# Half of the RWKV weight pieces split at use, low-rank outputs in two parts, other product rates

## Chip, cores and metric

The kernel runs on one core of a Trainium2 chip. The metric is device time in microseconds (us) of one execution. The profile shows one execution of the program: PE is the matmul engine (PEld its weight loads), DVE the vector engine, ACT the scalar engine, POOL GpSimd, and SP the engine whose queue issues most DMAs.

## What is computed

A two-layer trunk over 1024 tokens of width 1024, in float32. Layer 0 mixes tokens by a gated MLP (SGU), layer 1 by RWKV-7 time mixing; each is followed by a squared-ReLU MLP. Only the RWKV mixer and its products matter for the change:

```
xx = token_shift(h) - h
xr, xw, xk, xv, xa, xg = [h + xx * mu[i] for i in range(6)]
r, k, v = xr @ W_r, xk @ W_k, xv @ W_v             # "big": 1024 x 1024 each
w_log = -softplus(-(w0 + tanh(xw @ w1) @ w2)) - 0.5    # low rank: "hidden", then "outs"
a = sigmoid(a0 + (xa @ a1) @ a2)
g = sigmoid(xg @ g1) @ g2
y = wkv7_scan(r, exp(-exp(w_log)), k, v, -kk, kk * a)  # recurrence over tokens, 16 heads of 64
out = ((groupnorm(y) + bonus) * g) @ w_out          # "outp"
```

## The kernel before

**Three products for one.** Each float32 operand is split into a high part, rounded to the type fp32r, and a low part, the rest (`wh`, `wl` for weights). A product is high x high, high x low and low x high: three matmuls accumulate into one PSUM tile `acc`. A weight piece is one 128 x 512 tile (256 KB); twelve matmuls use it, two pieces make a block of eight row chunks.

**Where weight pieces come from.** `stream` lists the pieces in the order of use; `load_piece` loads up to three ahead; `split_piece` makes a piece ready, two pieces ahead of its use. There are two kinds. A raw piece is loaded as one tile `raw`, cast to `wh` (L401: two on ACT, the third on DVE) and subtracted to `wl` (L407: DVE and POOL in turn). A kept piece needs none of this: its two parts lie in DRAM (`split`), and `load_split` loads both (L326). The kept parts are made by `presplit` (L305 load, L355 cast on ACT, L358 subtraction on POOL, L336 two stores), step by step beside the layer-0 MLP. All 80 RWKV pieces are kept: 48 of r, k, v, 8 hidden, 8 outs, 16 of the output product.

**Stages of the RWKV mixer.** Tokens are worked in four quarters q of 256. `jobs` lists the products of a quarter: "big" products v, r, k, each in four parts m, with a hidden product behind m = 1 and all outs behind m = 2 (w beside v, a beside r, g beside k); after the four quarters come the output products "outp" of q = 0 and 1. The jobs of q = 0 run with raw pieces beside the end of the layer-0 MLP (about 1060 to 1220 us). All later ones run beside the recurrence (`wkv`), with kept pieces (1220 to 1810 us), followed by the first half of the layer-1 MLP with raw pieces, still beside the recurrence (to 2340 us).

**Results on their way.** Each job part m copies its PSUM tile into one of three `ev` buffers on ACT (L931 for big, L985 and L989 for outs) and ACT's queue stores it to DRAM (`sdr`, `sda`, ...). The recurrence loads these later. Only two PSUM tiles `acc` are open to products in this stage. When the output product of a quarter begins, `gated` loads its finished recurrence outputs (`ev<-yd`, L995) and splits them into `s`.

**The recurrence.** It has 16 units (4 quarters x 4 parts m). A unit moves its triangular matrix through DRAM: `ltd<-la`, `lb<-ltd` (L1412), a solve in many small DVE steps `pr`, `tb` (L1418 to L1424), `tpd<-tb` (L1428), `t<-tpd` and `pf<-tpd` (L1433). Then come twelve steps that depend on each other, of small PE matmuls `c`, DVE and ACT copies (`S` L1551, `uv` L1540, `xs` L1526).

**Order of the work.** `interleave` sets PE's order: each unit step has a due time in units; each piece of product work advances the clock by its cost over `RATES`, so 28.0 cost units of products lie in each of the first 10 units and 41.5 in each later one. PE keeps this order as written (`Pinned`); a scheduler sets the order on ACT, DVE, POOL and SP, and each of these works through its queue in order.

Of the kernel before, what the change touches and what calls it, by code (L numbers as in the profile page):

```python
# [16 lines left out]
P = 128  # L17
# [91 lines left out]
class Trunk:  # L109
# [148 lines left out]
    def std(self, src):  # L258

        return [(src[:, h * 4:h * 4 + 4], 1, None) for h in range(2)]  # L260
# [68 lines left out]
    def presplit(self, todo, pool):  # L329

        nc = self.nc
        got, out = [], iter(())

        def store(parts, ts, rows):
            for p, t in zip(parts, ts):
                nc.sync.dma_start(p[:rows], t[:rows])  # L336
                yield

        todo = list(zip(todo, self.split_ahead))
        for n in range(len(todo)):  # L340
            while len(got) < min(3, len(todo) - n):
                src, rep, _ = todo[n + len(got)][0]
                raw = pool.tile([P, 512], F32, name="araw", bufs=4)
                if rep:
                    k, m = src.shape[1:]
                    view = raw[:, :k * rep * m].rearrange("p (k r n) -> p k r n", k=k, r=rep)
                    self.fetch(view, src, rep)
                    rows = P
                else:
                    rows = self.fetch(raw, src, rep)[1]  # L350
                got.append((raw, rows))
            (raw, rows), ((_, _, low), (parts, _)) = got.pop(0), todo[n]
            m = parts[0].shape[-1]
            hi = pool.tile([P, 512], F32, name="ada_acc", bufs=2)
            nc.scalar.copy(hi[:rows, :m].bitcast(F32R), raw[:rows, :m])  # L355
            lo = slice(0, rows) if low is None else low
            to = raw if low is None else hi
            nc.gpsimd.tensor_tensor(to[lo, :m].bitcast(F32R), raw[lo, :m], hi[lo, :m], ALU.subtract)  # L358
            yield
            for _ in out:  # L360
                pass
            yield
            out = store(parts, (hi[:, :m], raw[:, :m]), rows)
            yield
        for _ in out:
            pass

    def make_split(self, dp):

        self.whole = [p for kind in ("big", "hidden", "outs", "outp")  # L370
                      for p in self.pieces(j for j in self.jobs() if j[1] == 0 and j[0] == kind)]
        kept = []
        for n, (src, rep, low) in enumerate(self.whole):
            m = src.shape[1] * rep * src.shape[2] if rep else 512
            rows = P if rep else sum(s.shape[0] for s in src)
            parts = [dp.tile([P, m], F32, name=f"split{n}_{i}") for i in range(1 if low else 2)]
            kept.append((parts, rows))
        self.split_ahead = kept
        at = lambda kind, q: [j for j in self.jobs() if j[:2] == (kind, q)]
        place, n = {}, 0  # L380
        for kind in ("big", "hidden", "outs", "outp"):
            for _, _, name, m in at(kind, 0):
                k = len(list(self.pieces([(kind, 0, name, m)])))
                place[kind, name, m] = slice(n, n + k)
                n += k
        self.order_split = [p for kind, _, name, m in self.parts()[1] for p in kept[place[kind, name, m]]]

    def split_piece(self):

# [420 lines left out]
    def jobs(self):  # L810


        for q in range(self.NQ):
            for name, low in ("vw", "ra", "kg"):
                for m in range(4):
                    yield "big", q, name, m
                    if m in (1, 2):
                        yield ("hidden", "outs")[m - 1], q, low, 0
        for q in range(2):
            for m in range(4):  # L820
                yield "outp", q, "", m
# [7 lines left out]
    def pieces(self, jobs):  # L829

        a = self.a
        std = self.std
        for kind, q, name, m in jobs:
            if kind == "big":
                for e in range(2 * m, 2 * m + 2):
                    yield from std(a["w_in"]["rkv".index(name) * 8 + e])
            elif kind == "outp":
                for e in range(2 * m, 2 * m + 2):
                    yield from std(a["b_w_out"][e])
            elif kind == "hidden":  # L840
                if name == "g":
                    yield from std(a["b_g1"][:, :, :P])
                    yield from [(a["b_g1"][:, h * 4:h * 4 + 4, P:], 3, None) for h in range(2)]
                else:
                    yield from [(a[f"b_{name}1"][:, h * 4:h * 4 + 4], 2, None) for h in range(2)]
            else:
                for h in range(2):
                    cs = slice(h * 512, h * 512 + 512)
                    if name == "g":
                        yield [a["b_g2"][:P, cs]], 0, None  # L850
                        yield [a["b_g2"][P:, cs]] * 3, 0, slice(64, 96)
                    else:
                        yield [a[f"b_{name}2"][:, cs]] * 2, 0, None

    def load_h(self, q):
        nc, N = self.nc, self.N
# [102 lines left out]
                nc.scalar.copy(gh[:96, 2], s[:96])  # L959
                nc.vector.tensor_tensor(gh[32:64, 2], s[32:64], rd(gh[32:64, 2]), ALU.subtract)  # L960

    def outs(self, q, name, _):
        nc = self.nc
        bias = {"w": self.w0h, "a": self.a0h, "g": None}[name]
        for m in range(4):
            if m % 2 == 0:
                wh, wl = self.piece()
                if name == "g":
                    gst, _ = self.piece()
            ps, half = self.acc2()  # L970
            for z in range(2):
                e = m % 2 * 2 + z
                es = slice(e * P, e * P + P)
                if name == "g":
                    gh = self.hid[:, 1:]
                    ops = (wh[:, es], gh[:, 0]), (wh[:, es], gh[:, 1]), (wl[:, es], gh[:, 0]), (gst[:96, es], gh[:96, 2])
                else:
                    ops = (wh[:, es], self.hid[:, 0]), (wl[:, es], self.hid[:, 0])
                for n, (w, x) in enumerate(ops):
                    self.pe.matmul(half[z], w, x, start=n == 0, stop=n == len(ops) - 1)  # L980
            yield 0.4 * len(ops)

            def emit(ev):
                if bias is None:
                    nc.scalar.copy(ev, ps)  # L985
                    return
                for z in range(2):
                    e = m * 2 + z
                    nc.scalar.activation(ev[:, z * self.N:(z + 1) * self.N], half[z], AF.Tanh, bias=bias[:, e:e + 1], scale=0.5)  # L989
            self.out2(q, name, m, emit)  # L990
# [191 lines left out]


    SLOT = 1 / 13
    RATES = [28.0] * 10 + [41.5]

    def wkv(self, bg):

# [605 lines left out]
```

## Time and profile before

| what | value |
|---|---|
| median of 3 runs | 2800.86 us (2793.97 to 2807.12) |
| profiled execution, its own time | 2805.26 us |
| its span, first to last instruction | 2803.5 us |
| busy in the span: PE | 2613.3 us, 93% |
| DVE, ACT, POOL | 1638.3, 1146.9, 544.7 us (58, 41, 19%) |
| DMA moved | 483.67 MB, mean 173 GB/s |
| mean granted clock of PE | 0.969 of full speed |

PE is busy for 93% of the span, so what counts is the other 7%, the time at a lower clock, and what ends PE's waits. The views used below are the table of busy time by stretch, the table of who waited for whom, the groups of instructions by line, the DMA issues with their median time from issue to landing, and single instructions in order of time.

### The profile page before, as it was taken

What the parts mean: (1) busy time and instruction counts of PE and PEld (TensorE: products, weight loads), DVE (VectorE), ACT (ScalarE), POOL (GpSimd) and SP (SyncE); (2) the same over time, 40 slices, a digit from 0 to 9 for tenths busy, and PEclk for the clock granted to TensorE, in tenths of its full rate; (3) what the DMA queues carried; (4) which work ended last, traced back from release to release, by engine and by line L of the source; (5) the groups of instructions that cost most, each with busy time, mean ns of one, the idle gap of its engine ahead of it and who ended that gap; (6) DMA issues with size and microseconds to landing.
All of it is one profiled execution on the core that took longest, in us unless ns stands there. A gap on an engine that the chain in (4) does not pass through costs nothing.

```text
span 2803.5 us, 49454 instructions
## 1 busy us (share of the span) xinstructions
PE 2613.3 (93%) x19020; PEld 2152.6 (77%) x19020; DVE 1638.3 (58%) x3066; ACT 1146.9 (41%) x2074; POOL 544.7 (19%) x574
## 2 busy tenths in 40 slices
PE   6999999999999999787898997879999999999998
PEld 4788888877888788787787886777777778788887
DVE  7856775444333458866666663566667545744445
ACT  4523442333311344553454543464444334533333
POOL 1000000433300013431322231123334220100001
PEclk9999999999999999998999999899999999999999
DMA  7644545888711354788888889753333324333332
GB/s 279 211 142 128 167 155 163 274 278 255 237 49 49 91 165 138 241 291 261 260 284 265 270 289 274 211 149 110 104 104 100 91 86 151 103 109 94 95 94 83
DMA packets 369708, 483.67 MB, mean 173 GB/s; under 512 B 144320, under 2 KB 153536, under 8 KB 368704
## 3 DMA queue, kind: packets, MB, share of 16 engines
q1 hardware_dynamic: 354496, 454.18, 52.3%
q10 hardware_dynamic: 14976, 26.34, 2.5%
q8 instruction: 149, 2.44, 0.4%
q14 instruction: 87, 0.71, 0.1%
HBM read 390.07 MB, written 90.32 MB: 171 GB/s over the span
## 4 chain that ended last, share of the span: by engine, by line
PE 67%; DVE 12%; DMA 11%; ACT 4%; issue 4%; SPq 1%; POOL 1%; ACTq 0%; DVEq 0%; POOLq 0%
PE acc L448 24%; PE acc L646 15%; PE acc L103 15%; PE c L103 2%; PE acc L503 2%; DMA split<-ada_acc 2%; PE t L103 2%; DMA split<-araw 2%; DVE pr L1420 2%; DVE hm L874 2%; PE acc L894 1%; DVE wl L407 1%; DMA araw<-in_ada_w 1%; DVE xi L440 1%; DMA lb<-ltd 1%
## 5 line engine op out<-in xcount | busy, mean ns | idle before, releaser
L448 PE MATMUL acc<-h,wh 128*128 128x512 f32 x2112 | 667.4, 397 | 0.0
L401 ACT CAST wh<-raw 128x512 fp32r<-128x512 f32 x517 | 318.6, 619 | 732.6 <-PE acc L448 299.0
L646 PE MATMUL acc<-s,wh 128*128 128x512 f32 (+1 forms) x1664 | 510.4, 389 | 12.1 <-DVE s L439 9.1
L407 DVE TENSOR_TENSOR wl<-raw,wh 128x512 fp32r<-128x512 f32 x475 | 363.1, 767 | 264.4 <-ACT wh L401 259.3
L448 PEld LDWEIGHTS acc<-h,wh 128*128 128x128 f32 x2112 | 394.9, 188 | 94.5 <-issue 1.2
L448 PE MATMUL acc<-h,wl 128*128 128x512 f32 x1056 | 418.0, 396 | 0.0
L646 PEld LDWEIGHTS acc<-s,wh 128*128 128x128 f32 x1664 | 308.9, 189 | 86.5 <-DVE s L439 14.8
L646 PE MATMUL acc<-s,wl 128*128 128x512 f32 (+1 forms) x832 | 323.1, 389 | 0.5 <-DVE wl L407 0.5
L452 DVE SCALAR_TENSOR_TENSOR x<-acc,mod,x 128x512 f32<-128x512 f32 (+1 forms) x224 | 163.1, 730 | 231.0 <-PE acc L646 206.4
L448 PEld LDWEIGHTS acc<-h,wl 128*128 128x128 f32 x1056 | 198.4, 188 | 48.0 <-issue 0.5
L103 PE MATMUL acc<-s,wh 128*128 128x512 f32 (+1 forms) x616 | 188.0, 390 | 35.0 <-ACT s L437 18.3
L407 POOL TENSOR_TENSOR wl<-raw,wh 128x512 fp32r<-128x512 f32 (+1 forms) x107 | 145.6, 1363 | 318.2 <-ACT wh L401 156.2
L103 PE MATMUL acc<-xi,wh 128*128 128x256 f32 (+1 forms) x896 | 179.5, 300 | 10.0 <-ACT hm L954 5.2
L646 PEld LDWEIGHTS acc<-s,wl 128*128 128x128 f32 x832 | 157.5, 189 | 35.3 <-DVE wl L407 1.2
L358 POOL TENSOR_TENSOR araw<-araw,ada_acc 128x512 fp32r<-128x512 f32 (+1 forms) x78 | 101.2, 1300 | 389.4 <-ACT ada_acc L355 354.1
L103 PEld LDWEIGHTS acc<-s,wh 128*128 128x128 f32 x616 | 111.0, 196 | 62.8 <-ACT s L437 18.8
L103 PEld LDWEIGHTS acc<-xi,wh 128*128 128x128 f32 (+1 forms) x896 | 144.3, 198 | 17.7 <-ACT hm L954 5.4
L103 PE MATMUL acc<-h,wh 128*128 128x512 f32 (+1 forms) x512 | 150.7, 381 | 3.2 <-ACT ev L1057 3.2
L103 PE MATMUL acc<-xi,wl 128*128 128x256 f32 (+1 forms) x448 | 129.8, 290 | 1.6 <-issue 0.8
L355 ACT CAST ada_acc<-araw 128x512 fp32r<-128x512 f32 (+1 forms) x80 | 49.4, 618 | 168.4 <-DMA split<-ada_acc 124.3
L103 PE MATMUL acc<-s,wl 128*128 128x512 f32 (+1 forms) x308 | 114.9, 373 | 0.0
L157 DVE SCALAR_TENSOR_TENSOR ada_acc<-araw,cond,ada_acc 128x512 f32<-128x512 f32 x140 | 104.4, 746 | 13.0 <-DMA araw<-in_ada_w 11.1
(269 smaller groups left out, 4415.8 us busy)
## 6 DMA issues: line engine op xcount, KB each, us to landing
raw<-in_mlp_w SPq DMA_DIRECT2D x432, 256.0 KB, 2.7
araw<-in_ada_w SPq DMA_DIRECT2D x192, 256.0 KB, 3.5
raw<-split SPq DMA_DIRECT2D x142, 256.0 KB, 4.9
wh<-split SPq DMA_DIRECT2D x141, 256.0 KB, 4.6
wl<-split SPq DMA_DIRECT2D x141, 256.0 KB, 4.7
split<-ada_acc SPq DMA_DIRECT2D x76, 256.0 KB, 3.8
split<-araw SPq DMA_DIRECT2D x76, 256.0 KB, 4.1
araw<-in_w_in SPq DMA_DIRECT2D x48, 256.0 KB, 3.8
```

What stands on the lines that cost most here:

```text
L103: self.tc.keep_in_program_order(self.pe.matmul(*a, **k))
L157: nc.vector.scalar_tensor_tensor(acc, raw, self.cond[:, k:k + 1], acc, ALU.mult, ALU.add)
L355: nc.scalar.copy(hi[:rows, :m].bitcast(F32R), raw[:rows, :m])
L358: nc.gpsimd.tensor_tensor(to[lo, :m].bitcast(F32R), raw[lo, :m], hi[lo, :m], ALU.subtract)
L401: (nc.vector.tensor_copy if self.nhi % 3 == 0 and self.shared else nc.scalar.copy)(wh[:rows], raw[:rows])
L407: eng.tensor_tensor(wl[:rows], raw[:rows], rd(wh[:rows]), ALU.subtract)
L448: nc.tensor.matmul(ps, w[s](k), x[m][:, k], start=n == 0, stop=n == 3 * KC - 1)
L452: self.nc.vector.scalar_tensor_tensor(x[:, e], ps, gate[:, e:e + 1], x[:, e], ALU.mult, ALU.add)
L503: self.nc.tensor.matmul(ps, h[s][:, k, ts], self.wv[k][m], start=k + i == 0, stop=k + i == KC + 1)
L646: nc.tensor.matmul(ps, w[:, k], s[hf, k][:, i, ts], start=n == 0, stop=n == 3 * FB - 1)
L874: nc.vector.scalar_tensor_tensor(t[:, z], self.hx[:, e + z], self.mu[:, i, e + z:e + z + 1], self.h[:, e + z, 1:], ALU.mult, ALU.add)
L1420: V.tensor_tensor(pr[:, :i, :i], lb[:, 0:i, i].unsqueeze(1).to_broadcast([64, i, i]), tb[:, 0, 0:i, 0:i].rearrange("p s k -> p k s"), ALU. ...
```

## The change

Of the 80 pieces, those with an odd number in the list that are plain 128 x 512 loads (the second half of each block of r, k, v and the output product, and one of g's hidden pieces, 33 in all) are no longer kept split. `presplit` leaves them out, and later quarters load them raw and split them at use. The outs of a low-rank product become two jobs of two parts each, one behind m = 2 and one behind m = 3. The rates become 27.3 for the first 10 units and 42.5 after them.

```diff
-        todo = list(zip(todo, self.split_ahead))
+        todo = [p for n, p in enumerate(zip(todo, self.split_ahead)) if n not in self.again]
...
+        self.again = {n for n, p in enumerate(self.whole) if p[1] == 1 and n % 2}
...
-        self.order_split = [p for kind, _, name, m in self.parts()[1] for p in kept[place[kind, name, m]]]
+        self.order_split = [self.whole[n] if n in self.again else kept[n]
+                            for kind, _, name, m in self.parts()[1]
+                            for n in range(place[kind, name, m].start, place[kind, name, m].stop)]
...
                 for m in range(4):
                     yield "big", q, name, m
-                    if m in (1, 2):
-                        yield ("hidden", "outs")[m - 1], q, low, 0
+                    if m:
+                        yield "outs" if m > 1 else "hidden", q, low, max(m - 2, 0)
...
-                for h in range(2):
-                    cs = slice(h * 512, h * 512 + 512)
+                cs = slice(m * 512, m * 512 + 512)
...
-    def outs(self, q, name, _):
+    def outs(self, q, name, part):
...
-        for m in range(4):
-            if m % 2 == 0:
-                wh, wl = self.piece()
-                if name == "g":
-                    gst, _ = self.piece()
+        wh, wl = self.piece()
+        if name == "g":
+            gst, _ = self.piece()
+        for m in range(2 * part, 2 * part + 2):
...
-    RATES = [28.0] * 10 + [41.5]
+    RATES = [27.3] * 10 + [42.5]
```

Counted over the whole program, PE issues the same matmuls. SP issues 190 DMAs of 256 KB fewer (1822 to 1632): 33 loads and 66 stores fewer in `presplit`, and 91 pieces loaded as one tile and not as two. In the stage beside the recurrence 91 casts (60 on ACT, 31 on DVE) and 91 subtractions (46 on DVE, 45 on POOL) are new; beside the layer-0 MLP 33 casts on ACT and 33 subtractions on POOL are gone.

What moves shows best at one place on ACT, and at one on SP and PE. On ACT it is the w outputs of q = 1 (`ev` holds a result, `sdw` and `sdv` are the stores to DRAM, L989 and L991 make the outputs). Before, from the first output's store to the third's:

```order
L922 DMA sdw1_8590<-ev_10822 128x512
L989 ACTIVATE ev_10840<-acc_10826,bvec_8527 128x256
L1399 COPY uv0_10446<-t_10836 64x2x128
L922 DMA sdw1_8590<-ev_10840 128x512
L1400 COPY uv0_10446<-t_10836 64x2x128
L989 ACTIVATE ev_10858<-acc_10848,bvec_8527 128x256 x2
L989 ACTIVATE ev_10871<-acc_10862,bvec_8527 128x256
L922 DMA sdw1_8590<-ev_10858 128x512
```

On ACT now, from the end of the first part to the start of the second:

```order
L991 ACTIVATE ev_10626<-acc_10610,bvec_8296 128x256
L1323 ACTIVATE g1_10788<-wa_10532 128x8x64
L925 DMA sdw1_8359<-ev_10626 128x512
L1388 COPY tm0_10214<-r_10667 128x512
L1344 ACTIVATE r_10531<-r_10531,bvec_8296 128x256 x2
L441 CAST xi_10804<-hm_8282 128x512
L441 CAST xi_10827<-hm_8282 128x512
L1401 COPY uv0_10215<-t_10703 64x2x128
L1402 COPY uv0_10215<-t_10703 64x2x128
L405 CAST wh_10738<-raw_10683 128x512
L934 COPY ev_10733<-acc_10630 128x512
L991 ACTIVATE ev_10749<-acc_10742,bvec_8296 128x256
```

Four outputs used to follow each other closely; now they come two and two, each pair behind a big product's copy (L934), with other work and the new cast of a weight piece (L405) in between.

The second place is where the output product of q = 0 begins. On SP's queue (`hm<-xd` loads the residual stream, `ev<-yd` the recurrence outputs, `tpd<-tb` stores a solved triangle), before:

```order
L326 DMA wh<-split_0_231 128x512
L1428 DMA tpd_257<-tb 64x16x16 x2
L326 DMA wl<-split_1_232 128x512
L1133 DMA hm<-xd 128x1024
L1433 DMA t<-tpd_257 64x8x64 x2
L1433 DMA pf_17741<-tpd_257 64x8x64 x2
L1133 DMA hm<-xd 128x1024 x3
L995 DMA ev<-yd_8607 128x512 x3
L326 DMA raw<-split_0_233 128x512
```

On SP now:

```order
L1430 DMA tpd_257<-tb 64x16x16 x2
L326 DMA wl<-split_1_226 128x512
L326 DMA wh<-split_0_225 128x512
L1435 DMA t<-tpd_257 64x8x64 x2
L1435 DMA pf_17588<-tpd_257 64x8x64 x2
L326 DMA raw<-split_0_229 128x512
L326 DMA raw<-split_1_230 128x512
L305 DMA raw<-in_b_w_out 128x512
L997 DMA ev<-yd_8376 128x512 x3
L326 DMA wh<-split_0_233 128x512
```

The four `hm<-xd` loads have left this place; they stand 26 to 66 rows further up.

On PE, the first matmuls of this product (`acc<-s`) stood ahead of the small matmuls `t<-t,la` that need that triangle: 48 of them had gone by when it came. Before:

```order
L103 MATMUL acc<-s,wh 128x256 x2
L103 MATMUL acc<-s,wl 128x256
L103 MATMUL c<-uv_16076,la_16077 64x64 x4
L103 MATMUL c<-S,ar_10432 64x64 x4
L103 MATMUL t<-t,la_16936 32x16 x32
L103 MATMUL acc<-s,raw 128x256 x12
```

On PE now:

```order
L103 MATMUL acc<-hr,wh 128x256
L103 MATMUL c<-uv_15895,la_15896 64x64 x4
L103 MATMUL c<-S,ar_10201 64x64 x4
L103 MATMUL t<-t,la_16756 32x16 x32
L103 MATMUL acc<-s,wh 128x256 x2
L103 MATMUL acc<-s,wl 128x256
```

The product now starts behind `t<-t,la`, and the last thing ahead of it is g's second pair of outputs (`hr`), no longer a big product. The output product of q = 1 has moved against the recurrence in the same way, and on SP its `ev<-yd` loads now stand behind the next unit's `tpd<-tb`, `t<-tpd` and `pf<-tpd`, where they stood ahead of them.

## Rows read from the trace of the kernel before

**Rows 1.** Busy time by stretch; behind the five engines the clock, DMA share and GB/s.
```profile
1060.00:1220.00 160.00, 136.43 (x858) 122.47 (x859) 128.08 (x186) 77.64 (x140) 69.20 (x54) 0.91 0.64 200
1220.00:1810.00 590.00, 502.92 (x6625) 452.99 (x6623) 347.31 (x866) 279.54 (x551) 141.30 (x173) 0.92 0.87 272
1950.00:2200.00 250.00, 242.82 (x2495) 184.97 (x2494) 166.12 (x366) 108.73 (x211) 97.70 (x104) 0.99 0.38 103
```
**Rows 2.** PE's waits, 1220 to 1810 us: us in total, times, longest.
```profile
PE acc L103 <- ACT s L437: 20.2, 3, 17.2
PE acc L103 <- ACT ev L989: 10.8, 8, 3.0
PE t L103 <- DMA t<-tpd: 9.8, 2, 9.4
PE c L103 <- DVE S L1551: 9.5, 8, 2.7
PE c L103 <- ACT uv L1540: 6.4, 4, 3.0
PE acc L103 <- ACT ev L931: 5.3, 5, 2.8
...
PE acc L103 <- DMA wh<-split: 2.1, 3, 0.9
```
**Rows 3.** SP's waits in the same stretch.
```profile
SPq L326 <- PE acc L103: 104.5, 120, 8.3
```
**Rows 4.** PE, in order of time, where q = 0's output product begins: start, us.
```profile
1751.08 1.31 PE L103 MATMUL acc<-s,wh 128*128 128x256 f32 x2 [17.18 <-ACT s L437]
...
1766.99 0.73 PE L103 MATMUL t<-t,la 16*32 16x16 f32 x64
```
**Rows 5.** SP there, in order of time.
```profile
1733.99 1.30 SPq L1428 DMA_DIRECT2D tpd<-tb  x2
...
1740.95 2.63 SPq L1133 DMA_DIRECT2D hm<-xd  x3
1743.68 1.52 SPq L995 DMA_DIRECT2D ev<-yd  x3
```
**Rows 6.** DMA issues, 1220 to 1750 us: count, KB each, median us to landing.
```profile
raw<-split SPq DMA_DIRECT2D x121, 256.0 KB, 5.0
...
lb<-ltd SPq DMA_DIRECT2D x9, 64.0 KB, 4.5
```
**Rows 7.** The same view, 1950 to 2300 us.
```profile
raw<-in_mlp_w SPq DMA_DIRECT2D x84, 256.0 KB, 2.8
...
lb<-ltd SPq DMA_DIRECT2D x5, 64.0 KB, 2.6
```
**Rows 8.** DVE's wait for a DMA, 1220 to 1810 us.
```profile
DVE tb L1418 <- DMA lb<-ltd: 25.6, 6, 6.2
```
**Rows 9.** Casts and subtractions of weight pieces, 1950 to 2200 us: busy us, mean ns.
```profile
L407 DVE TENSOR_TENSOR wl<-raw,wh 128x512 fp32r<-128x512 f32 x29 | 24.6, 850 | 4.5 <-ACT wh L401 3.8
...
L401 DVE CAST wh<-raw 128x512 fp32r<-128x512 f32 x20 | 10.0, 501 | 14.8 <-PE acc L103 8.0 <-issue 6.7
...
L407 POOL TENSOR_TENSOR wl<-raw,wh 128x512 fp32r<-128x512 f32 x29 | 39.6, 1365 | 75.6 <-ACT wh L401 34.9 <-PE acc L103 27.0 <-PE c L103 7.5
...
L401 ACT CAST wh<-raw 128x512 fp32r<-128x512 f32 x39 | 24.1, 618 | 52.4 <-PE acc L103 42.2 <-issue 7.3 <-POOL bk L1329 2.8
```
**Rows 10.** DVE's subtraction with little on POOL (200 to 400 us).
```profile
L407 DVE TENSOR_TENSOR wl<-raw,wh 128x512 fp32r<-128x512 f32 x56 | 38.0, 686 | 16.2 <-ACT wh L401 16.2
```
**Rows 11.** The same with POOL subtracting beside it (500 to 740 us).
```profile
L407 DVE TENSOR_TENSOR wl<-raw,wh 128x512 fp32r<-128x512 f32 x39 | 47.9, 1229 | 56.1 <-ACT wh L401 54.7 <-DMA split<-ada_acc 1.4
```
**Rows 12.** PE's waits, 1060 to 1220 us, where every piece is raw.
```profile
PE acc L894 <- DVE wl L407: 10.1, 9, 2.7
```
**Rows 13.** The high parts' stores of `presplit`: count, ns, first and last start.
```profile
L336 SPq DMA_DIRECT2D split<-ada_acc x80: 319/422/1607, 490.2 to 755.7; - x80
```
**Rows 14.** PE's wait beside `presplit`, 600 to 800 us.
```profile
PE acc L646 <- DVE s L439: 3.9, 1, 3.9
```

More of the change, by code (lines that the diff above doesn't have):

```diff
@@ L846, in pieces @@
             else:
-                for h in range(2):
-                    cs = slice(h * 512, h * 512 + 512)
-                    if name == "g":
[L850 to L853, printed above, removed]
+                cs = slice(m * 512, m * 512 + 512)
+                if name == "g":
+                    yield [a["b_g2"][:P, cs]], 0, None
+                    yield [a["b_g2"][P:, cs]] * 3, 0, slice(64, 96)
+                else:
+                    yield [a[f"b_{name}2"][:, cs]] * 2, 0, None
     def load_h(self, q):
@@ L960, in hidden @@
                 nc.vector.tensor_tensor(gh[32:64, 2], s[32:64], rd(gh[32:64, 2]), ALU.subtract)
-    def outs(self, q, name, _):
+    def outs(self, q, name, part):
         nc = self.nc
         bias = {"w": self.w0h, "a": self.a0h, "g": None}[name]
-        for m in range(4):
-            if m % 2 == 0:
-                wh, wl = self.piece()
-                if name == "g":
-                    gst, _ = self.piece()
+        wh, wl = self.piece()
+        if name == "g":
+            gst, _ = self.piece()
+        for m in range(2 * part, 2 * part + 2):
             ps, half = self.acc2()
```

## Prediction

> **What bounds the kernel now.** I read the busy time by stretch first. Almost everywhere PE is the bound; the stretch with room is 1220 to 1810 us, where products with kept weight pieces run beside the recurrence: PE is busy for 502.9 of 590 us at a mean granted clock of 0.92 (between the levels of 1.2 and 2.4 GHz), and DMA engines are at 0.87 [rows 1]. So 87 us are idle, and 0.08 x 590 = 47 us are what the lower clock costs. By contrast, 1950 to 2200 us, also beside the recurrence but with raw pieces, has PE at 242.8 of 250 us, clock 0.99 and DMA at 0.38 [rows 1].
>
> Then I read who ended PE's waits in that stretch [rows 2]. Few wait for a weight load: 2.1 us for the largest such row. The rest is of three kinds. One is the start of the output products, 20.2 us, of which 17.2 in one wait. The second is results that cannot leave: 10.8 + 5.3 = 16.1 us for `ev` copies. The third is the recurrence: 9.8 + 9.5 + 6.4 = 25.7 us for `t<-tpd`, `S` and `uv`. Behind the third stands DMA latency: DVE, which works in order, waited 25.6 us for `lb<-ltd` [rows 8], and everything behind it on DVE (`uv`, `S`) is late with it. That load took 4.5 us to land, against 2.6 us later; 256 KB weight loads took 5.0 against 2.8 [rows 6, 7]. SP is mostly ahead: it waited 104.5 us for PE to free weight buffers [rows 3].
>
> **The change part by part.** The sum is made against the profiled execution's 2805.3 us (span 2803.5 and 1.8 around it).
>
> *Outs in two parts.* Four outputs in a row need four `ev` buffers where there are three, just after a big product took one. ACT then waits for a store to land, and PE for its PSUM tile. Two at a time, behind one big copy, fit in three buffers. Of the 16.1 us [rows 2] I leave 5 for what other lateness on ACT causes: **-11** (bounds 0 and -16). The same matmuls are issued, so nothing is added.
>
> *Start of the output products.* For q = 0, PE stood still for 17.2 us until 1751.1 [rows 4]. SP stored the triangle at 1734.0 and only at 1743.7 issued the loads of recurrence outputs [rows 5], behind four `hm<-xd` loads of 512 KB; then landing, ACT's cast and DVE's subtraction followed. Now those loads are issued earlier, and PE gets there later: behind `t<-t,la`, which stood 1767.0 - 1751.1 = 15.9 us of PE's work behind the product's start [rows 4]. From the triangle's store I estimate about 7 us to the issue (9.7 less the 2.6 of the last three `hm<-xd` [rows 5]), 5 to land (as the 256 KB loads of [rows 6]) and 1.5 for cast and subtraction [rows 9], some 13.5 us. Without the stall PE was at the product's start when the store was issued; 15.9 us, less the few in which it was slowed by the wait behind it, leave it some 11 to 15 us after the store. I take 3 us left: **-14**. Bounds are -17 and +3, the latter since q = 1's loads now stand behind a triangle's store too.
>
> *Fewer bytes.* In the stretch 91 pieces are loaded as one tile and not two: 91 x 0.262 MB = 23.9 MB of 590 us x 272 GB/s = 160 MB. DMA then stands between 0.87 and 0.38; it is nearer to the first, so latency falls by a part of the 4.5 to 2.6 us gap. I take a quarter of the waits it bears on (25.7 + 2.1 us): **-7**. Bounds are 0 (bursts matter, not the mean) and -20.
>
> *Splits at use.* The cost: 60 casts on ACT x 618 ns = 37.1 us; 31 casts on DVE x 501 ns = 15.5; 46 subtractions on DVE x 850 ns = 39.1; 45 on POOL x 1365 ns = 61.4 [rows 9]. DVE goes from 347 to 402 busy us in 590, ACT from 280 to 317. What hides them is PE's lead: a piece is split two pieces before use. The nearest rows for the weights alone are two. With 58 raw pieces in 250 us, one in 4.3 us [rows 9], PE was idle for 7.2 us from all causes [rows 1]. From 1060 to 1220 us, where every piece is raw (72, one in 2.2 us), 10.1 us of PE's waits are for DVE's subtraction alone [rows 12], which for 91 pieces is 13. Here one comes in about 6 us, so I take 0 to 5. The larger part is what stands behind them: `S`, `uv` and the solve on DVE, `xs` on ACT; PE's next recurrence step waits for these. Of 37.1 + 15.5 + 39.1 = 91.7 us on ACT and DVE, I let 11 reach PE. Together **+16**, bounds 0 and 60. Raw loads on SP also wait for a buffer that a subtraction frees, and the recurrence's DMAs are queued behind them; SP has 91 DMAs fewer to issue here, so I count that as nothing.
>
> The Trainium skill (GPSIMD Engine Reference, Specifications) says that GpSimd shares its SBUF interfaces with VectorE and contends with vector instructions that read two SBUF operands; both kinds of subtraction are of that sort, so by this rule the change makes POOL and DVE slow each other. The trace agrees: DVE's subtraction took 686 ns with POOL idle and 1229 ns beside POOL's own [rows 10, 11]. By the worse duration the 46 subtractions would be 56.5 us and not 39.1, and at the same share on the path the term would be +18.
>
> *Clock.* In the stretch, 87 us of idle time stand beside 47 us lost to the clock, 0.54 us for each. Net idle time is -11 - 14 - 7 + 16 = -16, so **-9**.
>
> *`presplit`.* It loses 33 of 80 pieces: 33 ACT casts, 33 POOL subtractions, 99 DMAs. PE is nearly full there, so only its waits count. The stores last from 490.2 to 755.7 us [rows 13]; with 47 pieces at the same steps they end near 490 + 265 x 47/80 = 646. The wait of 3.9 us between 600 and 800 [rows 14], near 690 us, falls away with its clock: **-5** (bounds 0 and -12).
>
> *Rates.* In the first 10 units 7 cost units of products move behind the recurrence's first part, and into the later stretch, where PE is at 97% busy. The end of the recurrence in product units stays (10 x 27.3 + 7.65 x 42.5 = 598 against 280 + 7.65 x 41.5 = 597), so I take **0**, and 8 either way.
>
> Sum: -16 - 9 - 5 = -30. From 2805.3 this gives 2775; the median of the runs is 4.4 us below the profiled one, so **2771 us** as a median.
>
> **Rivals.** *DMA is the bound of the stretch.* Then time goes with the bytes: 23.9 MB at 272 GB/s is 88 us, and 2805.3 - 88 - 4.4 gives 2713. For it: DMA at 0.87 and landing times nearly doubled. Against it: 2.1 us in PE's largest wait for a weight load, and SP waiting for PE [rows 2, 3]. Chance 0.08.
>
> *The waits are dealt out again.* The new order moves every recurrence step against the products, and q = 1's loads now stand behind a triangle's store on SP. If one wait like q = 0's arises at q = 1, it costs 17.2 x 1.54 = 26 us, and -30 becomes -4: 2797. For it: that order is just the one that made the 17.2 us. Against: at q = 1 PE arrives later too. Chance 0.19.
>
> *DVE and ACT become late, and the kernel slower.* If the added 91.7 us stand mostly ahead of `S`, `uv` and `xs`, PE waits at each recurrence step. With x us on the path the whole is (x - 32) x 1.54 - 5. It is slower by over 14 us, 0.5%, from x = 44, just under half of the 91.7. At 0.6, x = 55: +30, so 2831. For it: these engines work in order, and DVE goes to 68% busy in a stretch that waits for it already. Against: 1950 to 2200 us has DVE at 166 of 250 us, 66%, and ACT at 43%, and PE waits little [rows 1]. Chance 0.15.
>
> *The change does not do what it says*: the order of instructions shows the 190 DMAs gone, so no chance is given to it.
>
> **How the numbers follow.** My forecast, 2771, has 0.58. Its own range, from the bounds, is 2740 to 2795. Some 0.5%, 14 us, is what a measurement of this kernel can tell from no change. Of the forecast's 0.58 I place 0.56 below 2787 and 0.02 within 0.5%. Faster: 0.56 + 0.08 = 0.64. Same: 0.02 + 0.19 = 0.21. Slower: 0.15. The range reaches down to 2730, past most of what a larger part of the latency gap would give, and up to 2812; it leaves out most of the DMA-bound case and most of the slow one.
>
> **What would show it.** In the profile after, between about 1210 and 1790 us: the row of PE's waits for `ev` at about 5 us; the wait at the first `acc<-s` under 5 us; DVE's wait for `lb<-ltd` clearly below 25.6 us and its landing below 4.5; DMA share near 0.78; few waits of PE for `wl` or `wh`; the clock above 0.92; and the last `presplit` store near 646 us. I am wrong if PE's waits for `S`, `uv` or `xs` grow past 30 us together, if a long wait stands at q = 1's first `acc<-s`, or if the stretch shortens by 70 us or more.

## The result, and the profile after

The changed kernel takes 2821.4 us (median of 6 runs, 2813.5 to 2829.3) against 2803.1 for the kernel before, taken with it: a ratio of 1.0066, 95% interval 1.0045 to 1.0087. It is 0.7% slower, some 18 us, where 1.1% faster was forecast; the range ended at 2812. The profiled execution took 2824.23 us, with a span of 2822.1. DMA moves 433.83 MB and not 483.67.

Busy time by stretch, answering [rows 1] (stretch and length, then PE, PE's loads, DVE, ACT, POOL, each with its instructions; granted clock, DMA share, GB/s):

```profile
1060.00:1220.00 160.00, 131.62 (x878) 118.04 (x878) 124.41 (x181) 77.61 (x139) 67.66 (x53) 0.95 0.64 198
1220.00:1810.00 590.00, 496.43 (x6405) 447.69 (x6403) 390.48 (x879) 295.95 (x583) 208.36 (x211) 0.89 0.75 225
1950.00:2200.00 250.00, 242.99 (x2358) 186.04 (x2357) 160.34 (x361) 109.93 (x210) 91.65 (x98) 0.97 0.38 103
```

The loss stands in the second line. DMA has its room, 0.75 and not 0.87. But PE is idle for 94 us and not 87, and its clock fell from 0.92 to 0.89, further from the upper level; POOL has 67 us more to do, DVE 43. Marked out by the work, the same is seen: from the first product beside the recurrence to the first output product of q = 0 it was 528.7 us before (1222.4 to 1751.1) and is 563.9 now (1218.1 to 1781.9), 35 us more. Part of this is recurrence work that the new rates moved forward: PE does 6088 matmuls in that stretch now and 5974 before. So the stretch from the first product that reads `h` (1850.6 before, 1885.5 now) to the last recurrence step has less to do, and its 466.8 us became 452.8. From the first product beside the recurrence to the last `c<-S` the matmuls are the same 11491 in both kernels, and there 1087.3 us became 1111.9: 25 us more.

Who ended PE's waits there, answering [rows 2] (total, times, longest):

```profile
PE c L103 <- DVE S L1553: 16.1, 6, 4.2
PE t L103 <- DMA t<-tpd: 13.2, 6, 5.6
PE acc L103 <- POOL wl L411: 12.6, 6, 3.0
PE acc L103 <- ACT ev L991: 11.4, 5, 3.7
PE acc L103 <- DVE wh L405: 9.4, 3, 4.8
PE c L103 <- ACT uv L1542: 6.0, 6, 2.5
PE acc L103 <- ACT s L441: 5.4, 1, 5.4
PE acc L103 <- ACT ev L934: 4.2, 4, 3.5
...
PE acc L103 <- DVE wl L411: 2.2, 2, 1.4
```

New are the rows for `wl` and `wh`, 24 us together: PE comes to a piece that is not yet split. `S` has grown from 9.5 to 16.1. The long wait for `s` is down from 17.2 to 5.4. `ev` is where it was.

SP's waits from 1220 to 1800 us, answering [rows 3], where 104.5 us for PE was by far the longest row and none stood for a subtraction:

```profile
SPq L326 <- PE acc L103: 61.1, 55, 6.2
SPq L326 <- POOL wl L411: 57.1, 22, 5.8
SPq L326 <- DVE wl L411: 24.7, 11, 5.4
SPq L305 <- PE acc L103: 19.1, 15, 5.5
SPq L305 <- POOL wl L411: 16.6, 5, 8.4
```

SP, which issues every load in order, now stands for 74 us behind POOL's subtractions and for 25 behind DVE's: a raw tile comes free only when its piece is subtracted.

### The profile page after: what moved, and what is told of

It reads as the page before. It is cut to its first block, busy times and chain, and to the rows that moved or that the text cites. A ratio compares the mean times of both kernels' runs of the same rounds, so it can differ in the third digit from the quotient of the medians.

```text
span 2822.1 us, 49257 instructions
## 1 busy us (share of the span) xinstructions
PE 2626.9 (93%) x19020; PEld 2167.3 (77%) x19020; DVE 1691.8 (60%) x3142; ACT 1161.6 (41%) x2101; POOL 580.3 (21%) x586
## 2 busy tenths in 40 slices
DMA packets 343113, 433.83 MB, mean 154 GB/s; under 512 B 141280, under 2 KB 151520, under 8 KB 342112
## 5 line engine op out<-in xcount | busy, mean ns | idle before, releaser
L405 ACT CAST wh<-raw 128x512 fp32r<-128x512 f32 x578 | 356.6, 619 | 823.1 <-PE acc L452 311.6
L411 DVE TENSOR_TENSOR wl<-raw,wh 128x512 fp32r<-128x512 f32 x521 | 390.6, 752 | 275.2 <-ACT wh L405 265.6
L650 PE MATMUL acc<-s,wh 128*128 128x512 f32 (+1 forms) x1664 | 506.3, 386 | 3.5 <-ACT wh L405 1.8
L650 PEld LDWEIGHTS acc<-s,wh 128*128 128x128 f32 x1664 | 306.6, 188 | 75.6 <-DVE s L443 5.8
L411 POOL TENSOR_TENSOR wl<-raw,wh 128x512 fp32r<-128x512 f32 x152 | 207.3, 1366 | 446.2 <-ACT wh L405 257.6
L103 PE MATMUL acc<-xi,wh 128*128 128x256 f32 (+1 forms) x1080 | 226.9, 310 | 21.6 <-ACT ev L991 11.4
L103 PE MATMUL acc<-s,wh 128*128 128x512 f32 (+1 forms) x664 | 201.1, 388 | 19.8 <-ACT s L441 10.1
L103 PEld LDWEIGHTS acc<-xi,wh 128*128 128x128 f32 (+1 forms) x1080 | 183.6, 210 | 29.7 <-ACT ev L991 12.8
L103 PE MATMUL acc<-xi,wl 128*128 128x256 f32 (+1 forms) x540 | 163.2, 302 | 14.9 <-POOL wl L411 12.6
L103 PEld LDWEIGHTS acc<-s,wh 128*128 128x128 f32 x664 | 122.4, 201 | 46.1 <-ACT s L441 10.7
L103 PEld LDWEIGHTS acc<-xi,wl 128*128 128x128 f32 (+1 forms) x540 | 113.2, 210 | 17.2 <-POOL wl L411 14.2
L358 POOL TENSOR_TENSOR araw<-araw,ada_acc 128x512 fp32r<-128x512 f32 (+1 forms) x45 | 58.5, 1302 | 322.8 <-ACT ada_acc L355 305.9
L157 DVE SCALAR_TENSOR_TENSOR ada_acc<-araw,cond,ada_acc 128x512 f32<-128x512 f32 x140 | 104.5, 747 | 15.4 <-DMA araw<-in_ada_w 13.3
```

What stands on the lines that cost most here:

```text
L103: self.tc.keep_in_program_order(self.pe.matmul(*a, **k))
L157: nc.vector.scalar_tensor_tensor(acc, raw, self.cond[:, k:k + 1], acc, ALU.mult, ALU.add)
L405: (nc.vector.tensor_copy if self.nhi % 3 == 0 and self.shared else nc.scalar.copy)(wh[:rows], raw[:rows])
L411: eng.tensor_tensor(wl[:rows], raw[:rows], rd(wh[:rows]), ALU.subtract)
L650: nc.tensor.matmul(ps, w[:, k], s[hf, k][:, i, ts], start=n == 0, stop=n == 3 * FB - 1)
```

## The experiments

The change has three parts: outputs in two parts ("outs"), every other kept piece split again at use ("again"), and the two rates ("rates"). Ratios are against the kernel before; 0.001 is 2.8 us.

My theory A: the splits' work, on ACT, DVE and GpSimd, is the loss, and the other parts are gains or nothing. Rival B: the new order and rates deal the recurrence's waits out anew, and that is the loss. Rival C: it is the buffers and where the loads stand on SP, not the work. Within A, A1 is work on ACT and DVE ahead of the recurrence's steps, and A2 is GpSimd slowing DVE.

### The three parts alone

Each kernel is the one before with the hunks of one part of the diff above, and then two of the parts.

```diff
-                    if m in (1, 2):
-                        yield ("hidden", "outs")[m - 1], q, low, 0
+                    if m:
+                        yield "outs" if m > 1 else "hidden", q, low, max(m - 2, 0)
...
```

> Before with the low-rank outputs in two parts alone; weights stay kept split, rates as before. Theory A (the splits at use are the loss): this part on its own is a gain, ratio 0.993 to 0.998 (6 to 20 us less), with the long wait of 17 us at the first output product gone. Theory B (the new order deals the waits out again, and that is the loss): about 1.003 to 1.008, with the longer time between the first recurrence step and the output products that the changed kernel shows (+35 us).

1.0076 (1.0049 to 1.0103): a loss of 21 us, which my theory A had as a gain. Rival B's number is met, but not its sign: in the profiled execution, the fastest of the six, the stretch ahead of the output products takes 528.8 us, as before.

```diff
+        self.again = {n for n, p in enumerate(self.whole) if p[1] == 1 and n % 2}
...
+        self.order_split = [self.whole[n] if n in self.again else kept[n]
...
```

> Before with every other piece split at use alone; order and rates as before. Theory A: this part is the loss, ratio 1.006 to 1.012 (17 to 34 us more), with waits of TensorE for wh and wl and of SyncE for subtractions as in the changed kernel. Theory B: 0.994 to 1.000, since the bytes fall and the split is hidden; the 7 us of the shorter presplit are kept.

1.0108 (1.0085 to 1.0132): a loss of 30 us, as theory A.

```diff
-    RATES = [28.0] * 10 + [41.5]
+    RATES = [27.3] * 10 + [42.5]
```

> Before with the two rates alone (27.3 and 42.5). Theory A: within 0.997 to 1.003. Theory B: 1.003 to 1.008, because the recurrence's steps move against the products.

0.992 (0.9895 to 0.9945): a gain of 22 us, which neither theory had.

The edits of "again" and "outs" together:

> The changed kernel with the rates of before. Theory A: near the changed kernel, 1.003 to 1.008 (the gain of the outputs taken off the loss of the splits). Theory B with the rates as its cause: 0.990 to 0.998.

1.0098 (1.0071 to 1.0125), above what either theory gave. Those of "again" and "rates":

> The changed kernel with the low-rank outputs in one part, as before. If the parts add up: 1.0108 x 0.992 = 1.003. If the outputs in two parts are a gain beside the splits (again_outs was 0.001 below again): 1.006 to 1.009, above the changed kernel. If they are a loss there too, as outs alone was: 0.998 to 1.003.

0.9995 (0.9985 to 1.0006). Those of "outs" and "rates":

> The changed kernel with all weights kept split, as before. If the parts add up: 1.0076 x 0.992 = 1.000. If the loss of outs is one of where the recurrence's steps fall (theory B), the other rates deal them anew and it may be 0.990 to 0.996, as rates alone.

0.995 (0.9938 to 0.9963). So the parts don't add up: alone they would give +21 + 30 - 22 = +29 us, together they give +18, and "outs" with "again" gives 27 where the two alone would give 51. "Outs" costs 21 us on the kernel before, 8 beside the rates, 20 beside rates and splits, and -3, which is no difference by the intervals, beside the splits alone. "Again" costs from 6 us beside "outs", again inside the intervals, to 33 beside "outs" and "rates". Added in the order rates, splits, outputs, the parts give -22, +21 and +20 us. The profiled executions of these three steps, with the same 6088 matmuls from the first product beside the recurrence to the first output product, take 515.3, 544.6 and 563.9 us for that stretch.

### What of the splits costs: bytes or work

The split's work without its savings: the odd pieces are loaded as before, in both parts, and then cast and multiplied in place.

```diff
...
+        if len(self.wgot[0]) == 4:
+            wh, wl = self.wgot.pop(0)[:2]
+            self.nhi += 1
+            (nc.vector.tensor_copy if self.nhi % 3 == 0 else nc.scalar.copy)(wh, rd(wh))
+            self.nlo += 1
+            (nc.gpsimd if self.nlo % 2 == 0 else nc.vector).tensor_tensor(wl, rd(wl), rd(wh), ALU.mult)
+            self.wready.append((wh, wl))
+            return
```

> Before, with a cast of wh in place (ACT, every third on DVE) and a product of wl with wh in place (DVE and GpSimd in turn) on every other kept piece when it is used: the split's work with its chain, with the bytes, tiles and loads of before. Theory A (the work on DVE, ACT and GpSimd is the loss): 1.008 to 1.020, with waits of TensorE for wl, S and uv as in the changed kernel. Theory C (the loss comes from buffers and from where the loads stand on SyncE, not from the work): 0.998 to 1.005. The low part is spoilt by the product, so the output is not the reference's in its last digits.

1.0155 (1.0138 to 1.0171): 43 us for the work alone, in theory A's range; rival C, which had 0.998 to 1.005, is not the cause here, where loads and buffers are those of before. The opposite, the bytes saved and no work (the low part of every other kept piece is left out, and its high part is used for both):

```diff
+        if len(parts) > 1 and parts[0] is parts[1]:
+            t = self.load_split(parts[:1], rows)[0]
+            return t, t
...
```

> Before, with every other kept piece loaded as its high part alone, used for both parts (the low part is left out): the bytes of the changed kernel without any split at use. By my prediction's term for the bytes, 7 us less and up to 20 (0.993 to 1.000); if DMA bounds the stretch, 0.965 to 0.975; if landing times don't follow the mean load, 0.998 to 1.002.

0.9983 (0.9974 to 0.9991): the bytes are worth 5 us. That DMA bounds the stretch falls with this run. "Again" is +30, so 43 - 5 leaves some -8 for the shorter `presplit` and all else, a difference of three measured numbers.

### Whose work

The eight lines of "work" with the cast only, with GpSimd's products only, and with DVE's only (a product in place stands for the subtraction here as there):

```diff
...
+            self.nhi += 1
+            (nc.vector.tensor_copy if self.nhi % 3 == 0 else nc.scalar.copy)(wh, rd(wh))
```

> Of the work's three parts only the casts in place (two on ACT, one on DVE in turn), on every other kept piece; bytes, tiles, order as before. The whole work was 1.0155. Theory A1 (ACT and DVE late ahead of the recurrence's steps, by their added time): cast takes 37 + 15 of 92 us there, so 1.007 to 1.010. Theory A2 (GpSimd's port contention with DVE): 1.000 to 1.004.

1.0064 (1.0044 to 1.0085), 18 us.

```diff
...
+            self.nlo += 1
+            if self.nlo % 2 == 0:
+                nc.gpsimd.tensor_tensor(wl, rd(wl), rd(wh), ALU.mult)
```

> Of the work only the products in place on GpSimd, on every fourth kept piece; nothing added on ACT and DVE. Theory A1: 1.000 to 1.003, since GpSimd is off the recurrence's path there and has room. Theory A2: 1.006 to 1.012, with DVE's own operations longer than before.

1.0079 (1.0059 to 1.0098), 22 us.

```diff
...
+            if self.nlo % 2 != 0:
+                nc.vector.tensor_tensor(wl, rd(wl), rd(wh), ALU.mult)
```

> Of the work only the products in place on DVE, on every fourth kept piece. Theory A1: 39 of 92 us, 1.006 to 1.008. Theory A2: 1.001 to 1.004, as the DVE time alone is hidden.

1.0048 (1.0032 to 1.0064), 13 us. The three make 53 us against 43 for all at once. The one that adds nothing to ACT or DVE costs no less than the others, in theory A2's range; the other two cost too, each between what A1 and what A2 gave it, so neither theory is the whole. Busy time from 1220 to 1750 us in three kernels: before, with GpSimd's products, with DVE's (columns as above):

```profile
1220.00:1750.00 530.00, 454.13 (x5996) 409.88 (x5994) 315.49 (x782) 252.09 (x499) 133.24 (x161) 0.93 0.88 277
```
```profile
1220.00:1750.00 530.00, 457.33 (x6000) 412.41 (x5998) 337.03 (x782) 252.67 (x499) 188.19 (x200) 0.94 0.85 271
```
```profile
1220.00:1750.00 530.00, 456.19 (x6003) 412.20 (x6002) 340.39 (x821) 251.82 (x499) 140.61 (x162) 0.94 0.86 275
```

In the second, DVE does its 782 instructions as before, and they take 21.5 us longer: 39 products on GpSimd cost DVE 0.55 us each. In the third DVE does 39 more instructions itself and is busy for 24.9 us more, 0.64 us each. By these two executions, handing a product to GpSimd saves DVE little. The groups show where: DVE's own `hm` and `pr` rows, with GpSimd's products beside them, and then before:

```profile
L888 DVE SCALAR_TENSOR_TENSOR hm<-hm,mu 128x256 f32<-128x256 f32 x132 | 76.8, 612 | 4.0 <-POOL hm L885 3.2
L1434 DVE TENSOR_TENSOR pr<-lb,tb 64x4 f32<-64x4 f32 (+6 forms) x126 | 57.4, 455 | 3.5
...
L407 POOL TENSOR_TENSOR wl<-wl,wh 128x512 fp32r<-128x512 f32 x26 | 39.8, 1532 | 71.7 <-DMA wl<-split 36.8 <-DMA raw<-split 11.3 <-PE m L103 9.6
```
```profile
L874 DVE SCALAR_TENSOR_TENSOR hm<-hm,mu 128x256 f32<-128x256 f32 x132 | 68.6, 549 | 5.0 <-POOL hm L871 4.2
L1420 DVE TENSOR_TENSOR pr<-lb,tb 64x4 f32<-64x4 f32 (+6 forms) x126 | 50.2, 398 | 3.4
```

`hm` goes from 549 to 612 ns, `pr` from 398 to 455; with `xi` (716 to 752) these rows hold 18 of the 21.5 us. `S` itself stays at 274 ns, but PE's wait for it goes from 9.5 to 16.2 us (12.6 with DVE's products). PE also waits for GpSimd's products themselves (1220 to 1810 us):

```profile
PE c L103 <- DVE S L1565: 16.2, 10, 3.5
...
PE acc L103 <- POOL wl L407: 4.5, 3, 2.0
```

So DVE's longer operations are one way in which GpSimd's products cost time, and late pieces are another; how the 22 us divide between them was not measured.

### The remedy that this points to

If GpSimd is the loss, the changed kernel must gain when DVE gets all subtractions, although DVE has more to do.

```diff
-            eng = nc.gpsimd if self.nlo % 2 == 0 and self.shared or self.nlo <= 8 else nc.vector
+            eng = nc.gpsimd if self.nlo % 2 == 0 and self.shared and not self.steps or self.nlo <= 8 else nc.vector
...
+    steps = False
...
+        self.steps = True
```

> The changed kernel with every subtraction of a weight on DVE from the recurrence's start on, none on GpSimd. Theory A2 (GpSimd slows DVE's own operations): per piece the work cost 22 us / 45 on GpSimd and 13 / 46 on DVE, so 9 us less for the kept pieces alone and up to 20 with the raw ones behind them: 0.999 to 1.0035 against 1.0066. Theory A1 (DVE's time ahead of the recurrence's steps): DVE has 31 us more, 1.008 to 1.012.

0.9945 (0.9931 to 0.9959): 34 us faster than the changed kernel, and faster than before. What theory A1 gave for this run fails: DVE has 15 us more from 1220 to 1750 us and the kernel is quicker. (That added work on ACT and DVE costs too stays shown by the casts and by DVE's products.) The gain is also more than the 20 us I had given theory A2. First its stretch as above, then PE's waits from 1220 to 1800 us, SP's there, and two groups (busy us, mean ns):

```profile
1220.00:1750.00 530.00, 462.23 (x6056) 416.76 (x6058) 373.88 (x888) 281.66 (x556) 149.32 (x165) 0.93 0.78 239
```
```profile
PE t L103 <- DMA t<-tpd: 21.4, 6, 8.9
PE acc L103 <- ACT ev L991: 10.4, 5, 4.7
PE c L103 <- DVE S L1555: 9.2, 6, 3.0
...
PE acc L103 <- DVE wl L411: 3.3, 5, 1.3
```
```profile
SPq L326 <- PE acc L103: 71.9, 69, 4.2
SPq L326 <- DVE wl L411: 54.3, 28, 4.8
```
```profile
L877 DVE SCALAR_TENSOR_TENSOR hm<-hm,mu 128x256 f32<-128x256 f32 x132 | 67.9, 544 | 9.1 <-POOL hm L874 8.8
L411 DVE TENSOR_TENSOR wl<-raw,wh 128x512 fp32r<-128x512 f32 x76 | 57.8, 762 | 28.2 <-ACT wh L405 27.0
```

The same groups of the changed kernel:

```profile
L877 DVE SCALAR_TENSOR_TENSOR hm<-hm,mu 128x256 f32<-128x256 f32 x128 | 76.6, 629 | 5.6 <-POOL hm L874 5.1
L411 DVE TENSOR_TENSOR wl<-raw,wh 128x512 fp32r<-128x512 f32 x36 | 30.9, 857 | 6.5 <-ACT wh L405 6.0
...
L411 POOL TENSOR_TENSOR wl<-raw,wh 128x512 fp32r<-128x512 f32 x36 | 50.0, 1388 | 79.6 <-ACT wh L405 35.2 <-DVE wh L405 27.0 <-DMA wl<-split 10.0
```

Two things come together. DVE's own operations are short again (`hm` 629 to 544 ns), and PE's wait for `S` is at 9.2. And a piece that took 1388 ns on GpSimd takes 762 on DVE: SP's 74 us behind GpSimd's subtractions are gone (behind DVE's it stands for 54 and not 25), and PE's waits for `wl` and `wh` went from 24 to under 4 us. PE's wait for `t<-tpd` grew, from 13.2 to 21.4. The second thing could show only in part in the experiments on the kernel before, as no load there waited for a subtraction; how the 34 us divide between the two was not measured. The two profiled executions are 36 us apart: 29 of them stand ahead of the first output product (563.9 us and 534.6, the same 6088 matmuls), and 11 between the first product that reads `h` and the last `c<-S` (444.4 and 433.3).

The same edit where no kept piece is split:

> The kernel of the two rates alone (0.992) with every subtraction of a raw weight on DVE from the recurrence's start on. These stand behind 1800 us mostly, where TensorE is 97% busy, so little is to be had there: theory A2 0.988 to 0.992, theory A1 0.993 to 0.998.

0.9891 (0.9873 to 0.9909). The raw pieces behind some 1800 us alone give some 8 us (0.9891 against 0.992), a difference that lies inside the two intervals; this is the fastest kernel of the study, 31 us below the one before. The edit with two parts of the change at a time completes a square, the edits of "again" and "rates", and of "outs" and "rates":

> The changed kernel with the outputs in one part as before, and every subtraction on DVE from the recurrence's start on (after_dve was 0.9945). If the outputs in two parts are a loss of some 8 us by themselves: 0.991. If they only deal the waits out anew, anything from 0.985 to 0.998. Against rates_dve (0.9891) it shows what the splits cost without GpSimd: with 53 + 27 us on ACT and DVE and 12 us given back by bytes and presplit, 0.989 to 0.995.

0.9918 (0.9898 to 0.9938).

> The changed kernel with all weights kept split, and every subtraction of a raw piece on DVE from the recurrence's start on. outs_rates was 0.995, and the subtractions gave 0.003 in rates_dve: 0.992. Against after_dve (0.9945) it shows what the splits cost without GpSimd: a gain if it stands above 0.9945.

0.9925 (0.9902 to 0.9947). Without subtractions on GpSimd the parts add up: on 0.9891 the splits cost 0.0027, the outputs 0.0034, and both 0.0054. The splits' price is 8 us (6 beside "outs"), where with GpSimd it was 21 (again_rates against rates) and 33 (the change against outs_rates). The outputs' price beside rates and splits falls with it too, from 20 us to 8. The intervals are as wide as these 6 to 10 us, so what is shown is that the splits stopped being a large loss, not that they are a small one.

### Is the gain of the rates a slope?

```diff
+    RATES = [26.6] * 10 + [43.5]
```

> Before with the rates moved twice as far, 26.6 and 43.5. Rates of 27.3 and 42.5 gave 0.992. If the gain is one of fewer products beside each early step of the recurrence, it goes on: 0.984 to 0.990. If it is an accident of where the steps fall, anything from 0.990 to 1.005; a spread of that size among near neighbours speaks for the accident.

0.998 (0.9965 to 0.9994).

```diff
+    RATES = [27.65] * 10 + [42.0]
```

> Before with the rates moved half as far, 27.65 and 42.0. Rates gave 0.992 at 27.3 and 0.998 at 26.6. If there is a broad valley around 27.3: 0.992 to 0.997. If the gain is an accident of one dealing: 0.998 to 1.006.

0.9984 (0.9969 to 0.9998). So 28, 27.65, 27.3 and 26.6 give 0, -4, -22 and -6 us: not a slope, and no broad valley. That 27.3 is a place where the recurrence's steps happen to fall well among the products is argued from this scatter; no run shows which steps. The same step of the rates gave -32 beside the splits, -35 beside "outs" and -9 beside both.

### A second look at the outputs in two parts

The kernel "outs" once more, unaltered, since its first profiled execution was its fastest (2806.8 us):

> A second profile of the kernel with the outputs in two parts alone, since its first profiled execution was its fastest (2807 against a median of 2822). Where the 15 us more stand: if between the first recurrence step and the output products, the loss is one of the recurrence's dealing; if before it, one of the raw stage, where the outputs' second part stands behind another big product.

2818.6 us in one execution. Against its first profile, 6 of the 12 us stand ahead of the first product that reads `xi` (1061.6 and 1055.5 us), where both are the same program and "outs" has not begun; 5 in the raw stage behind it (173.2 and 168.7), 8 between the first product beside the recurrence and the output products (536.4 and 528.8), and 6 are given back later. Two executions of one kernel settle little, but the raw stage (the products of q = 0) can be read in all twenty profiled executions. With the same 890 matmuls it takes 168.7 to 173.7 us in the seven executions with the outputs in two parts, and 164.1 to 167.5 in the thirteen without. Some 5 us of this part's price stand there; the rest is not placed.

## Why the prediction was wrong

**Splits at use: +16 forecast, some +43 measured for their work.** This is the first of the two steps that failed. With its share of the clock's term +16 is 25 us (16 x 1.54), so it misses by 18 to 27 of the 48 us that lie between -30 and +18. I wrote that PE's lead hides the work: 0 to 5 us for pieces that are not ready, and 11 of the 91.7 us on ACT and DVE for what stands behind them. POOL's 61.4 us got no price of their own.

In the changed kernel PE waits 24 us for `wl` and `wh` where I had 0 to 5, and half of that for GpSimd. The stretch that I took for it had shown this. From 1060 to 1220 us PE waited 10.1 us for DVE's subtractions, which I counted [rows 12], and 7.7 for GpSimd's, which I did not:

```profile
PE acc L894 <- POOL wl L407: 7.7, 7, 3.1
```

The waits for `S` and `uv`, the other half of the term, grew from 15.9 to 22.1 us together, within the 11. On the kernel before, the casts cost 18 us, GpSimd's products 22, DVE's 13. The bounds (0 to 60) held the 43. The rival "DVE and ACT become late" had the outcome, at 0.15, but not the way: its sign, `S`, `uv` and `xs` past 30 us together, did not come. What I set against it, that DVE at 66% does no harm from 1950 to 2200 us, did not carry over: there 41.5 cost units of products stand beside each recurrence step and here 28, so PE has less to do here while a step is late. That reading is argued, not measured; that the work costs here is measured.

The Trainium skill (GPSIMD Engine Reference, Specifications) was the rule that spoke against the change, and the trace agrees with it beyond what I took from it. I priced it as a longer subtraction on DVE, +2 us. What it cost was other operations of DVE: 0.55 us of DVE's time for each product given to GpSimd, most of it in `hm`, `pr` and `xi`, which read two SBUF tiles each; `S`, which reads one result of PE, stayed at 274 ns.

**SP's buffers, counted as nothing.** SP waited 74 us for GpSimd's subtractions and 25 for DVE's. I had named this wait, set SP's 91 DMAs fewer against it, and counted nothing; what it costs by itself was not measured. A load that waits for a subtraction, which waits for a cast, which waits for PE to free `wh` (10.8 us on DVE alone), ties the engines to each other in both directions.

**Outs in two parts: -11 forecast, between -3 and +21 measured, +20 beside rates and splits.** This is the second step that failed, by as much as the first. Half of the mechanism was right: ACT's waits for a store behind `ev`, 12.6 us over six rows before, are gone. But PE's waits for `ev` stayed, at 16.2 us, since what is late next on ACT is something else. One place shows it, ACT in order of time (start, us, operation):

```profile
1646.78 0.58 ACT L934 COPY ev<-acc 128x512 f32<-128x512 f32 x1
...
1648.04 1.28 ACT L1326 ACT_TABLE_LOAD   x1
1649.33 0.69 ACT L1326 ACTIVATE rn<-m,tiny 128x512 f32<-128x512 f32 x1
1650.03 1.28 ACT L991 ACT_TABLE_LOAD   x1
1651.32 1.20 ACT L991 ACTIVATE ev<-acc,bvec 128x256 f32<-128x256 f32 x3
```

PE waits 3.7 us until 1652.2 for this `ev`, behind a norm of the recurrence with a table load on either side of it. I had left 5 us "for what other lateness on ACT causes"; it was all 16. Some 5 us of this part's price stand in the raw stage; why the rest of the 8 to 21 us in most pairs is there stays open.

**Start of the output products: -14 forecast, -12 in that wait.** The wait is 5.4 us and not 17.2, and `t<-t,la` stands ahead of the product now, as the order had shown [rows 4]:

```profile
1775.80 0.72 PE L103 MATMUL t<-t,la 16*32 16x16 f32 x64
1781.94 1.31 PE L103 MATMUL acc<-s,wh 128*128 128x256 f32 x2 [5.41 <-ACT s L441]
```

Half of the reasoning held: PE is ready for the product at 1776.5, 12.6 us after the triangle's store, where I had 11 to 15. The other half did not. The loads of the recurrence outputs were not issued earlier, some 7 us behind that store, but 13.3, against 9.7 before [rows 5]:

```profile
1763.94 2.54 SPq L1430 DMA_DIRECT2D tpd<-tb  x2
...
1777.20 4.24 SPq L997 DMA_DIRECT2D ev<-yd  x3
```

From that issue to the product it took 4.7 us and not the 6.5 of my sum, or the 7.4 of before, so the size came out near by luck. A second wait for `s` of 4.0 us has come behind it, at 1840.8. All waits for `s` there make 20.2 us before, 18.9 with "outs" alone, 15.0 with "again", 18.3 with "rates", 9.3 with "again" and "rates" and 10.1 with all: it came with splits and rates together, not with the outputs in two parts.

**Fewer bytes: -7 forecast, -5 measured.** The size was near, but not by the way that I gave: `lb<-ltd` takes 4.8 us to land and not less than 4.5, though the DMA share fell to 0.75 and whole pieces land in 4.4 [rows 6]:

```profile
raw<-in_w_in SPq DMA_DIRECT2D x68, 256.0 KB, 4.4
...
lb<-ltd SPq DMA_DIRECT2D x9, 64.0 KB, 4.8
```

DVE's wait for it fell from 25.6 to 13.8 us all the same [rows 8]. But with the fewer bytes alone, where they were worth 5 us, it rose (1220 to 1810 us), so the near size was luck:

```profile
DVE tb L1425 <- DMA lb<-ltd: 48.5, 10, 7.5
```

**Clock: -9 forecast; it got worse.** With idle time not falling, the clock fell from 0.92 to 0.89 in the stretch. The signs rested on the sum, which had the wrong sign.

**`presplit`: -5 forecast, some -10 measured.** The last store of the high parts begins at 646.9 us (646 forecast), and the wait near 690 us [rows 14] is gone. The first product that reads `xi` begins 7 us earlier (1055.4 and 1048.3). That point alone moves by 6 us between two executions of one program, but it stands between 1042.4 and 1050.8 us in the six profiled executions with the shorter `presplit`, and between 1053.9 and 1062.4 in the fourteen without.

**The waits dealt out again.** This rival had its long wait at q = 1, and none came: from 1900 us on no wait of PE's is over 2 us. That a new order can move the time by as much, the next point shows, with up to 35 us; that dealt-out waits are the cause is argued.

**Rates: 0, 8 either way, forecast; -22 alone and -9 to -35 beside the others.** The cost units at the recurrence's end were the wrong thing to look at. The end stands where it stood among the products; what changed is how much PE waits on the way. From the first product beside the recurrence to the last `c<-S`, the same 11491 matmuls, PE was idle for 117 of 1087 us before and for 94 of 1056 with the rates alone.

Of the signs I had named, `ev` at 5, few waits for `wl` and `wh`, the clock and the landing of `lb` failed; DMA share, the start of the output products nearly, DVE's wait for `lb` and the last store held.

## What to carry to other kernels

A stretch in which PE, DVE and ACT wait for each other in turn has little cover for work "beside" it: here the casts, GpSimd's products and DVE's each cost some 40 to 53% of the busy time that they added from 1220 to 1750 us (18 of 34 us, 22 of 55, 13 of 25), though every engine but PE was under 70% busy. When the nearest stretch is read for a price, take in the waits for every engine that does the work. Before work is shared between DVE and GpSimd, see what GpSimd costs DVE (rows of the same DVE instruction with and without it); where the answer is nearly the whole operation, GpSimd is no second engine, only a slower one. Parts of a change that move a hand-made order differed by some 20 us here by what stood beside them, so a part is judged beside the others, not alone.

## What the runs showed of the hardware

- A 128x512 product on GpSimd took 1.5 us and raised DVE's busy time by 0.55; on DVE it took 0.69 us and raised DVE's busy time by 0.64 (39 products each, 1220 to 1750 us).
- The time of a 64 KB load to land did not follow the mean DMA share: 4.5 us at 0.88 and 4.8 at 0.75, from 1220 to 1750 us.
- The same program reached the same product at 1055.5 us in one execution and at 1061.6 in another.
